# A two-layer hybrid trunk: the normalised input of the zm, gp and gm projections is formed once more from the reloaded residual

## The chip, the cores and the metric

The kernel runs on one core of a Trainium2 chip. The metric is device time in microseconds (us) for one execution. The kernel before took 788.91 us, the median of three runs (788.84 to 789.22).

Five engines work side by side, each through its own instructions in order: TensorE (PE, with its weight loads listed as PEld), VectorE (DVE), ScalarE (ACT), GpSimd (POOL) and SyncE (SP, which here only issues transfers). They meet through semaphores; TensorE writes to accumulator banks (PSUM), from which VectorE or ScalarE take the result away.

## The reference

Two layers, 512 tokens and 16 meta tokens in front of them (528 in all), model width 1024:

```python
for l in range(DEPTH):                       # DEPTH = 2
    h = rmsnorm(h_res, norm_gain[l])         # x * inv * gain, inv = rsqrt(mean(x*x) + eps)
    proj = h @ w_in[l]
    u_pool, z_pool, c_q, c_kv, k_rope, z_mla, g_pool, g_mla = split(proj)   # 512, 512, 768, 256, 32, 512, 1024, 1024
    y_pool = (pool_mix(u_pool, ...) * silu(z_pool)) @ pool_w_up[l]
    o_mla = mla(c_q, c_kv, k_rope, ...)      # 8 heads, q and k normalised, causal softmax
    y_mla = (o_mla * silu(z_mla)) @ mla_w_up[l]
    merged = sigmoid(g_pool) * y_pool + sigmoid(g_mla) * y_mla
    h_res = h_res + merged @ w_out[l]
return h_res[:, N_META:]
```

All of it is fp32.

## The kernel before

**Layout and arithmetic.** Features lie on the 128 partitions and tokens along the free dimension. Layer 0 computes 528 tokens in two segments of 264 (`FULL`), layer 1 only the 512 real tokens where it can (`XTOK`). Each fp32 operand of a projection is split into a high and a low half, and `mm3` (lines 184 to 187) makes each product of three matmuls: high by high (L185), low by high (L186), high by low weight (L187).

**The trunk.** `register` lists the projections of a layer in order, as `Gemm` entries: ckv, cq, u, k, v, zp (the pool branch's z), y, qr and qn (the query projection), pu0 to pu7 (the pool branch's up projection), zm0 to zm3 (the latent attention's z), gp and gm (the two gates, eight blocks each), mu (the attention's up projection) and o. The generator `stream` emits their matmuls. The weights come through `wload` (L170 to 182): a 256 KB transfer on SP's queue into one of three `raw` buffers, the high half by ScalarE (L180), the low half by VectorE (L181), three buffers of each.

**Order.** A planner clock `clk` counts the emitted matmuls at their nominal time. `fill_now(ns)` emits trunk matmuls until the clock has moved by ns, `upto(name)` until a projection is done, and `after(ns, fn)` puts work off to a due time. The source order that results is handed to a scheduler, which reorders each engine's instructions by a simulated timeline, within their dependencies.

**The norm.** `hbuf` (tiles hh and hl) holds the split of gain times x, without the factor `inv`, one value for each token. The factor is known only later (slot `rinv`, spread over the partitions), so it is applied when a result leaves PSUM. Three evacuations of the projections behind the query projection do so: `ev_silu` for zm (L505 multiplies by 0.5 and `inv`, ScalarE takes tanh, VectorE forms (tanh + 1) times that), `ev_gp` (L573: VectorE multiplies by `inv` into a temporary, ScalarE takes tanh of half of it, VectorE multiplies the pool branch's `am`), and `ev_gm` (L873 and ScalarE's tanh in place, into slot cq0 to cq7). The PSUM tiles that they read carry the tag mm (four banks); there are three of tag S and one o.

**Behind the query projection.** In `go`, after qn3, `qk_stats` (L665) sums the squares of queries and keys: matmuls into two S banks (`stat_go`, L453), `stat_rows` (ScalarE copy L463, VectorE add L464, once for each half of the tokens), 2.6 us of trunk, five small transposes on TensorE (L674, L675) and a Newton iteration on VectorE. Then 9.5 us of trunk, another 2.6, and `prep(0)`, which forms head 0's key (VectorE L701, GpSimd L702, the split L276 and L277 on ScalarE and VectorE) and moves parts of the query (L712). Then come the eight heads, with trunk matmuls filled in between: pu, zm, gp and part of gm. `part2` (L828) multiplies a head pair's output by zm, `meta_out` (L863) does so for the meta tokens, `ev_mu` (L877 ff.) joins the gates, `ev_o` forms the new residual and writes it to `scr` in memory and, in layer 0, to `xb`.

Slots cq0 to cq5 hold the query latent until the query projection has read it (cq6 and cq7 hold earlier squares), and later gm's gates.

Of the kernel before, what the change touches and what calls it, by code (L numbers as in the profile page):

```python
# [9 lines left out]
F32 = mybir.dt.float32  # L10
# [3 lines left out]
AF = mybir.ActivationFunctionType  # L14
ALU = mybir.AluOpType
# [3 lines left out]
P = 128  # L19
DEPTH = 2  # L20
D = 1024
SEQ = 512
NM = 16
T = SEQ + NM
# [13 lines left out]
MT_ZP = 6  # L38
MT_CQ = 10
MT_GP = 16  # L40
MT_ZM = 24
# [8 lines left out]
G_H, G_CKV, G_CQ, G_QN, G_QR, G_KN, G_KR, G_PS = 0, 8, 10, 16, 17, 18, 19, 20  # L50
# [21 lines left out]
def trunk(ctx, tc, xT, pos, win, wkr, wqb, wkb, wvb, wgr, wpu, wmu, wout, gains, const, yT):  # L72
    nc = tc.nc
    pe, act, dve, gp, sp = nc.tensor, nc.scalar, nc.vector, nc.gpsimd, nc.sync
# [7 lines left out]
    pp = ctx.enter_context(tc.tile_pool(name="pp", bufs=1, space=bass.MemoryType.PSUM))  # L82
# [3 lines left out]
    def nm(s):  # L86
        uid[0] += 1
        return f"{s}_{uid[0]}"

    def slot(tag, dt=F32, bufs=1, w=W):  # L90
        return sl.tile([P, w], dt, tag=tag, name=nm(tag), bufs=bufs)

    def tmp(w=W):
        return tp.tile([P, w], F32, tag="tmp", name=nm("tmp"), bufs=3)
# [1 line left out]
    def sqt():  # L96
        return tp.tile([P, HALF], F32, tag="sq", name=nm("sq"), bufs=14)

    def mmt():
        return pp.tile([P, 512], F32, tag="mm", name=nm("mm"), bufs=4)  # L100

    def sct():
        return pp.tile([P, 512], F32, tag="S", name=nm("S"), bufs=3)

    FULL = [(0, HALF), (HALF, T)]
    XTOK = [(NM, T)]
# [3 lines left out]
    xb = cp.tile([P, 8, W], F32, name="xb")  # L110
# [80 lines left out]
    done = set()  # L191

    def stream():
        flat = [(g_, c) for g_ in plan for c in range(0, g_.width, 512)]
        flat[1], flat[2] = flat[2], flat[1]

        def load(i):
            g_, c = flat[i]
            n = min(512, g_.width - c)
            return wload(g_.src[:, c:c + n], n, g_.gain, g_.spare)  # L200

        ahead = []
        for i in range(4):
            ahead.append(load(i))
            yield 0.0
        for i, (g_, c) in enumerate(flat):
            w = ahead.pop(0)
            if i >= 3 and i + 1 < len(flat):
                ahead.append(load(i + 1))
            final = c + 512 >= g_.width  # L210
            if g_.body is not None:
                yield from g_.body(c // 512, w)
            else:
                xs = g_.xs()
                K = len(xs)
                if c == 0:
                    g_.pss = [g_.alloc() for _ in g_.segs]
                k0 = c // P
                for ps, (a, b) in zip(g_.pss, g_.segs):
                    n = b - a  # L220
                    for k in range(k0, min(K, k0 + 4)):
                        o = (k - k0) * P
                        mm3(ps[:, :n], w[0][:, o:o + P], w[1][:, o:o + P],
                            xs[k][0][:, a:b], xs[k][1][:, a:b], k == 0, k == K - 1)
                        if k < K - 1 and (k - k0) % 2 == 1:
                            yield 6 * (n / 2.4)
                    if final:
                        g_.evac(ps[:, :n], a, b)
                        if b == g_.segs[-1][1]:
                            done.add(g_.name)  # L230
                        yield 6 * (n / 2.4)
            if final:
                done.add(g_.name)

    clk = [0.0]
    pend = []

    def step():
        c = next(main, None)
        if c is None:  # L240
            flush()
            return False
        clk[0] += c
        while pend and pend[0][0] <= clk[0]:
            pend.pop(0)[1]()
        return True
# [22 lines left out]

    def fill_now(ns):  # L270
        end = clk[0] + ns
        while clk[0] < end and step():
            pass

# [31 lines left out]
    scr = dp.tile([P, 8, SEQ], F32, name="scr")  # L306
# [6 lines left out]
    class Layer:  # L313
# [182 lines left out]
                dve.tensor_mul(self.us[m][:, NM + a:NM + b], ps, self.inv[:, a:b])  # L496
            return ev

        def ev_silu(self, dst, tag, m):
            def ev(ps, a, b):  # L500
                if a == self.x0:
                    dst[m] = slot(f"{tag}{m}") if tag == "u" else xb[:, m]
                d = dst[m][:, a:b]
                t = tmp()
                dve.scalar_tensor_tensor(out=d, in0=ps, scalar=0.5, in1=self.inv[:, a:b],  # L505
                                         op0=ALU.mult, op1=ALU.mult)
                act.activation(t[:, :b - a], d, AF.Tanh)
                dve.scalar_tensor_tensor(out=d, in0=t[:, :b - a], scalar=1.0, in1=d, op0=ALU.add, op1=ALU.mult)
            return ev

        def window(self, m):
# [58 lines left out]
        def ev_gp(self, m):  # L570
            def ev(ps, a, b):
                t = tmp()
                dve.tensor_mul(t[:, :b - a], ps, self.inv[:, a:b])  # L573
                act.activation(t[:, :b - a], t[:, :b - a], AF.Tanh, scale=0.5)
                dve.scalar_tensor_tensor(out=self.am[m][:, a:b], in0=t[:, :b - a], scalar=1.0,
                                         in1=self.am[m][:, a:b], op0=ALU.add, op1=ALU.mult)
            return ev
# [85 lines left out]
            return ev  # L663

        def qk_stats(self):  # L665
            fill_now(LAG + 100)
            self.stat_go(7)
            sts = self.stat_rows(self.x0)
            if self.last:
                dve.memset(sts[0:H, 0:NM], 1.0)  # L670
            fill_now(2600)
            stp = mmt()
            for j in range(4):
                pe.transpose(stp[:, H * j:H * j + H], sts[0:H, NM + P * j:NM + P * (j + 1)], ident[0:H, 0:H])  # L674
            pe.transpose(stp[0:NM, 4 * H:5 * H], sts[0:H, 0:NM], ident[0:H, 0:H])  # L675
            na, ny, nt = (sm.tile([P, 5, H], F32, tag=t, name=nm(t)) for t in ("na", "ny", "nt"))
            dve.memset(na[:, 4, :], 1.0)
            dve.tensor_scalar(self.eps, self.eps, EPS, None, op0=ALU.mult)
            eps = self.eps.unsqueeze(2).to_broadcast([P, 5, H])
            for r, j, k in ((P, 0, 4), (NM, 4, 5)):  # L680
                dve.scalar_tensor_tensor(out=na[0:r, j:k, :], in0=stp[0:r, H * j:H * k].rearrange("p (a b) -> p a b", b=H),
                                         scalar=1.0 / QK, in1=eps[0:r, j:k, :], op0=ALU.mult, op1=ALU.add)
            newton(ny, na, nt)
            self.nqs = sm.tile([P, 5, H], F32, tag="nqs", name=nm("nqs"))
            dve.tensor_scalar(self.nqs, ny, -1.0 / math.sqrt(QK), None, op0=ALU.mult)
            fill_now(9500)
            if not self.last:
                self.smeta = sm.tile([NM, 8, NM], F32, tag="smeta", name=nm("smeta"))

# [89 lines left out]
        def pv(self, prev, js):  # L779
# [3 lines left out]
            p, odd = h // 2, h % 2  # L783
# [8 lines left out]
            for j in js:  # L792
# [7 lines left out]
                out = ops[:, P * j:512]  # L800
# [17 lines left out]
            if odd == 1:  # L818
                op = self.op
                mt = self.mt  # L820

                def part2():
                    th, m = mt, mmt()
                    pe.matmul(m, self.vb[:, P * p:P * (p + 1)], th[0:96, 0:512], start=True, stop=True)
                    self.ogs[p] = (slot(f"q{p}", F32R), slot(f"kn{p}", F32R))
                    f = op[:, NM:T]
                    dve.tensor_add(f, m, f)
                    dve.tensor_mul(f, f, self.zms[p][:, NM:T])  # L828
                    split(*self.ogs[p], f, NM, T)

                after((3 if p == 3 else 2) * LAG, part2)
# [30 lines left out]

        def meta_out(self, p):  # L863
            f = tmp()
            dve.tensor_mul(f[:, 0:NM], self.mo[:, NM * p:NM * (p + 1)], self.zms[p][:, 0:NM])
            split(*self.ogs[p], f[:, 0:NM], 0, NM)

        def ev_gm(self, m):
            def ev(ps, a, b):
                if a == self.x0:  # L870
                    self.gms[m] = slot(f"cq{m}")
                d = self.gms[m][:, a:b]
                dve.tensor_mul(d, ps, self.inv[:, a:b])  # L873
                act.activation(d, d, AF.Tanh, scale=0.5)
            return ev

        def ev_mu(self, m):  # L877
# [31 lines left out]
        def register(self, nxt):  # L909
            l, XS = self.l, self.XS  # L910
            wi = lambda t: win[l, t]
            hs, ys, cs = (lambda: self.hs), (lambda: self.ys), (lambda: self.cs)

            def add(name, src, width, **kw):
                plan.append(Gemm((l, name), src, width, **kw))
# [16 lines left out]
                    add("kr", wkr[l], 256, body=self.kr_body, gain=gn[:, l * N_GAIN + G_H:l * N_GAIN + G_H + 8])  # L932
                kk(m)
            def zp(m):
                add(f"zp{m}", wi(MT_ZP + m), D, evac=self.ev_silu(self.zps, "xa", m), xs=hs, segs=XS)

            def y(m):
                add(f"y{m}", wgr[l, m], P, evac=self.ev_y(m), xs=lambda: [self.ys[m]], segs=XS)
# [15 lines left out]
            for m in range(8):  # L954
                add(f"pu{m}", wpu[l, m], 512, evac=self.ev_pu(m), xs=ys, segs=XS)
            for m in range(4):
                add(f"zm{m}", wi(MT_ZM + m), D, evac=self.ev_silu(self.zms, "u", m), xs=hs, segs=XS)
            for m in range(8):
                add(f"gp{m}", wi(MT_GP + m), D, evac=self.ev_gp(m), xs=hs, segs=XS)
            for m in range(8):  # L960
# [12 lines left out]
        def go(self, nxt):  # L973
# [29 lines left out]
                self.stat(self.acc[:, a0:b], a0, b, C_CQ, self.acc_last)  # L1003
            up("qn3")
            self.qk_stats()
            fill_now(2600)
            kq = self.prep(0)
            fill_now(2600)
            due[0] = None
# [100 lines left out]
```

## Time and profile before

| | |
|---|---|
| median of three runs | 788.91 us (788.84 to 789.22) |
| span of the profiled execution | 787.1 us |
| instructions | 14567 |
| matmuls on TensorE | 5301 |
| bytes moved by transfers | 81.83 MB |

The span goes from the first to the last instruction of one profiled execution; the median also has what lies around it. "Busy" is time in which an engine executes; the tenths of 40 slices show where in the span. A row of instructions reads: line of the kernel and engine, operation, result <- operands by the program's names, partitions x elements, how many, then busy time, mean duration in ns, and the idle time just before them with what ended most of it. A row of a timeline reads: start, duration, engine and line, operation, and in brackets a wait and what released it. A row by windows reads: the window, its length, and for each engine (TensorE, its weight loads, VectorE, ScalarE, GpSimd) the busy time and, in parentheses, the instructions; then the granted clock, the share of the transfers and their GB/s. A row of transfers ends with the KB of each and the median us from issue to landing.

Layer 0's last result leaves PSUM in a 0.42 us instruction that starts at 403.84 us (VectorE, L898); layer 1 takes the rest. The query projection's last evacuation (ScalarE, L661) starts at 149.85 us in layer 0 and at 542.8 us in layer 1.

### The profile page before, as it was taken

To read this page: it belongs to the slowest core of one execution; us is meant where nothing else is said; L and a number is where in the kernel's file an instruction comes from. 1 tells how busy PE (TensorE), PEld (TensorE's weight loads), DVE (VectorE), ACT (ScalarE), POOL (GpSimd) and SP (SyncE) were. 2 spreads that over 40 slices of the span, in tenths; PEclk is the share of its full clock that TensorE was granted. 3 is DMA by queue.
4 is the path that set the end of the run, shared out by engine and by line. 5 is a ranking of instruction groups with operands and counts; after the bars stand their busy time and mean duration, and the time that the engine had idled before them with its cause. 6 is when DMAs were issued, how large, how long until landed. Compare 5 with 4: busy or idle time off the path is not lost.

```text
span 787.1 us, 14567 instructions
## 1 busy us (share of the span) xinstructions
PE 780.9 (99%) x5301; PEld 708.6 (90%) x5301; DVE 535.1 (68%) x1165; ACT 410.8 (52%) x930; POOL 194.4 (25%) x259
## 2 busy tenths in 40 slices
PE   9999999999999999999999999999999999999998
PEld 8999899999999999999997898887788888887887
DVE  5848787446779987675464487775467888755932
ACT  7645655635656565633354356455445666554420
POOL 1034504002333242051000145131022333410500
PEclk9999999999999999999999999999999999999999
DMA  6242333423223212224642422334232222122372
GB/s 242 82 102 85 96 120 102 128 81 94 96 76 92 78 58 78 95 81 146 192 123 94 95 88 90 129 88 136 96 105 88 95 84 82 65 81 67 102 242 84
DMA packets 52263, 81.83 MB, mean 104 GB/s; under 512 B 8784, under 2 KB 17360, under 8 KB 52192
## 3 DMA queue, kind: packets, MB, share of 16 engines
q1 hardware_dynamic: 52048, 80.65, 32.9%
q8 instruction: 41, 0.67, 0.4%
q14 instruction: 30, 0.25, 0.1%
q10 hardware_dynamic: 144, 0.26, 0.1%
HBM read 74.49 MB, written 4.27 MB: 100 GB/s over the span
## 4 chain that ended last, share of the span: by engine, by line
PE 95%; DMA 2%; DVE 1%; issue 1%; ACT 0%; SPq 0%; ACTq 0%
PE mm L185 28%; PE mm L187 28%; PE mm L186 28%; PE mm L796 2%; PE S L186 2%; PE S L187 1%; PE S L185 1%; PE o L802 1%; PE o L801 1%; PE S L453 1%; DMA xb<-xT 1%; PE mm L355 1%; DVE wlo L181 1%; PE mm L412 0%; DMA rinv<-win 0%
## 5 line engine op out<-in xcount | busy, mean ns | idle before, releaser
L185 PE MATMUL mm<-hh,whi 128*128 128x264 f32 (+2 forms) x1096 | 346.7, 318 | 0.2 <-ACT racc L810 0.2
L186 PE MATMUL mm<-hl,whi 128*128 128x264 f32 (+2 forms) x1096 | 343.9, 315 | 0.0
L187 PE MATMUL mm<-hh,wlo 128*128 128x264 f32 (+2 forms) x1096 | 343.0, 315 | 0.0
L181 DVE TENSOR_TENSOR wlo<-raw,whi 128x512 fp32r<-128x512 f32 (+2 forms) x251 | 188.6, 755 | 119.6 <-ACT whi L180 115.9
L180 ACT ACTIVATE whi<-raw 128x512 fp32r<-128x512 f32 (+2 forms) x251 | 150.4, 601 | 187.5 <-PE mm L186 126.5
L185 PEld LDWEIGHTS mm<-hh,whi 128*128 128x128 f32 x1096 | 205.9, 188 | 13.6 <-ACT racc L810 0.5
L186 PEld LDWEIGHTS mm<-hl,whi 128*128 128x128 f32 x1096 | 206.6, 189 | 11.8
L187 PEld LDWEIGHTS mm<-hh,wlo 128*128 128x128 f32 x1096 | 205.5, 188 | 12.0
L774 POOL TENSOR_TENSOR pm<-pa,rs 128x16 f32<-128x16 f32 x32 | 11.6, 361 | 181.3 <-DVE rs L769 181.3
L560 POOL TENSOR_TENSOR racc<-racc,tmp 128x264 f32<-128x264 f32 (+1 forms) x15 | 14.2, 948 | 153.8 <-ACT tmp L559 129.8
L702 POOL TENSOR_TENSOR tmp<-kp,bc 64x528 f32<-64x528 f32 x16 | 22.5, 1408 | 76.9 <-PE mm L675 44.5
L884 POOL TENSOR_TENSOR tmp<-tmp,xb 128x264 f32<-128x264 f32 (+1 forms) x24 | 27.1, 1149 | 58.2 <-DVE tmp L882 33.1
L730 DVE CUSTOM_DVE_ANT_0 S<-S,maskw,nqs 128x272 f32<-128x272 f32 (+4 forms) x80 | 38.5, 498 | 4.2 <-PE S L187 3.9
L737 ACT ACTIVATE cq<-S,bia 128x400 f32<-128x400 f32 (+2 forms) x48 | 24.6, 516 | 22.6 <-DVE bia L764 12.0
L185 PE MATMUL mm<-u,whi 128*128 128x264 f32 (+1 forms) x108 | 35.2, 326 | 0.0
L187 PE MATMUL mm<-cq,wlo 128*128 128x264 f32 (+1 forms) x108 | 34.5, 323 | 0.7 <-DVE wlo L181 0.7
L187 PE MATMUL mm<-u,wlo 128*128 128x264 f32 (+1 forms) x108 | 34.8, 323 | 0.0
L185 PE MATMUL mm<-cq,whi 128*128 128x264 f32 (+1 forms) x108 | 34.6, 320 | 0.0
L186 PE MATMUL mm<-cq,whi 128*128 128x264 f32 (+1 forms) x108 | 34.5, 321 | 0.0
L277 DVE TENSOR_TENSOR tl<-mm,th 128x512 fp32r<-128x512 f32 (+1 forms) x64 | 29.3, 481 | 6.1 <-ACT th L276 5.1
L776 POOL TENSOR_TENSOR cq<-cq,rs 128x384 f32<-128x384 f32 (+1 forms) x32 | 32.8, 1025 | 0.0
L186 PE MATMUL mm<-kn,whi 128*128 128x264 f32 (+1 forms) x96 | 30.7, 321 | 0.0
(252 smaller groups left out, 1362.4 us busy)
## 6 DMA issues: line engine op xcount, KB each, us to landing
raw<-win SPq DMA_DIRECT2D x143, 256.0 KB, 2.6
raw<-wout SPq DMA_DIRECT2D x32, 256.0 KB, 2.7
bc<-kdr SPq DMA_DIRECT2D x16, 264.0 KB, 3.6
raw<-wpu SPq DMA_DIRECT2D x16, 256.0 KB, 2.7
raw<-wmu SPq DMA_DIRECT2D x16, 256.0 KB, 2.5
raw<-wqb SPq DMA_DIRECT2D x12, 256.0 KB, 2.6
tmp<-xT SPq DMA_DIRECT2D x16, 132.0 KB, 3.0
tmp<-scr SPq DMA_DIRECT2D x7, 256.0 KB, 3.4
```

The source lines that it names most:

```text
L180: act.activation(hi[:, :n], raw[:, :n], AF.Copy)
L181: dve.tensor_sub(lo[:, :n], raw[:, :n], hi[:, :n].bitcast(F32))
L185: pe.matmul(out, wh, xh, start=start, stop=False)
L186: pe.matmul(out, wh, xl, start=False, stop=False)
L187: newest[0] = pe.matmul(out, wl, xh, start=False, stop=stop)
L277: dve.tensor_sub(lo[:, a:b], src, hi[:, a:b].bitcast(F32))
L702: gp.tensor_mul(kf[r0:r0 + 64, :], self.kp[r0:r0 + 64, :], bc[r0:r0 + 64, :])
L730: dve.tensor_tensor_reduce(out=sv, in0=sv, in1=mask, scale=nqs[:, i, h:h + 1], scalar=3e38, op0=ALU.add, op1=ALU.min, accum_out=bia[:, c:c ...
L737: act.activation(pv, sv, AF.Exp, scale=-1.0, bias=bia[:, i:i + 1], accum_out=rs[:, c:c + 1])
L776: gp.tensor_mul(pt[i][:, NM:], pt[i][:, NM:], rs[:, i:i + 1].to_broadcast([P, n - NM]))
L796: pe.transpose(tr[:, P * (i - j):P * (i - j + 1)], pt[i][:, NM + P * j:NM + P * (j + 1)], ident)
L884: gp.tensor_add(t[:, :b - a], t[:, :b - a], self.am[m][:, a:b])
```

## The change

After the query projection the kernel reads its input again: x in layer 0 (`xT`), the stored residual in layer 1 (`scr`), one block of 128 features at a time into slots cq0 to cq7. It multiplies each block by `inv` and splits gain times that into the same hh and hl tiles. This is the new method `renorm`: per block one transfer on SP, a multiply on VectorE, a copy with gain on ScalarE and a subtract on VectorE. In the source six blocks come at the end of `qk_stats`, in place of its 9.5 us of trunk, and two behind it, in place of 2.6 us; they are set to planner times from the start of `qk_stats` (6.0 us and 1.5 us more for each block), through the new `fill_to`.

From zm on, the projections therefore come out normalised. The evacuations of gp and gm drop their multiply by `inv`, and ScalarE takes tanh from PSUM. That of zm takes tanh from PSUM and then forms (tanh + 1) times the PSUM value on VectorE; the factor 0.5, which used to lie in it, moves to the two places that read zm. PSUM tiles of the trunk are named by their projection.

```diff
+    def fill_to(end):
+        while clk[0] < end and step():
+            pass
...
+        def renorm(self, ks):
+            x0 = self.x0
+            assert (self.l, "pu7") not in done
+            for k in ks:
+                x = slot(f"cq{k}")
+                src = xT[:, k, x0:T] if self.l == 0 else scr[:, k, :]
+                sp.dma_start(x[:, x0:T], src)
+                x, (hh, hl), gk = x[:, x0:T], self.hs[k], self.g(G_H + k)
+                dve.tensor_mul(x, x, self.inv[:, x0:T])
+                act.activation(hh[:, x0:T], x, AF.Copy, scale=gk)
+                dve.scalar_tensor_tensor(out=hl[:, x0:T], in0=x, scalar=gk, in1=hh[:, x0:T].bitcast(F32),
+                                         op0=ALU.mult, op1=ALU.subtract)
+
+        def ev_zm(self, m):
+            def ev(ps, a, b):
+                if a == self.x0:
+                    self.zms[m] = slot(f"u{m}")
+                t = tmp()
+                act.activation(t[:, :b - a], ps, AF.Tanh, scale=0.5)
+                dve.scalar_tensor_tensor(out=self.zms[m][:, a:b], in0=t[:, :b - a], scalar=1.0, in1=ps,
+                                         op0=ALU.add, op1=ALU.mult)
             return ev
...
         def ev_gp(self, m):
             def ev(ps, a, b):
                 t = tmp()
-                dve.tensor_mul(t[:, :b - a], ps, self.inv[:, a:b])
-                act.activation(t[:, :b - a], t[:, :b - a], AF.Tanh, scale=0.5)
+                act.activation(t[:, :b - a], ps, AF.Tanh, scale=0.5)
...
         def qk_stats(self):
+            self.t0 = clk[0]
             fill_now(LAG + 100)
...
-            fill_now(9500)
+            for k in range(6):
+                fill_to(self.t0 + 6000 + 1500 * k)
+                self.renorm((k,))
...
                     dve.tensor_add(f, m, f)
-                    dve.tensor_mul(f, f, self.zms[p][:, NM:T])
+                    dve.scalar_tensor_tensor(out=f, in0=f, scalar=0.5, in1=self.zms[p][:, NM:T],
+                                             op0=ALU.mult, op1=ALU.mult)
...
         def meta_out(self, p):
             f = tmp()
-            dve.tensor_mul(f[:, 0:NM], self.mo[:, NM * p:NM * (p + 1)], self.zms[p][:, 0:NM])
+            dve.scalar_tensor_tensor(out=f[:, 0:NM], in0=self.mo[:, NM * p:NM * (p + 1)], scalar=0.5,
+                                     in1=self.zms[p][:, 0:NM], op0=ALU.mult, op1=ALU.mult)
...
         def ev_gm(self, m):
             def ev(ps, a, b):
                 if a == self.x0:
                     self.gms[m] = slot(f"cq{m}")
-                d = self.gms[m][:, a:b]
-                dve.tensor_mul(d, ps, self.inv[:, a:b])
-                act.activation(d, d, AF.Tanh, scale=0.5)
+                act.activation(self.gms[m][:, a:b], ps, AF.Tanh, scale=0.5)
             return ev
...
-                add(f"zm{m}", wi(MT_ZM + m), D, evac=self.ev_silu(self.zms, "u", m), xs=hs, segs=XS)
+                add(f"zm{m}", wi(MT_ZM + m), D, evac=self.ev_zm(m), xs=hs, segs=XS)
...
             self.qk_stats()
-            fill_now(2600)
+            for k in (6, 7):
+                fill_to(self.t0 + 6000 + 1500 * k)
+                self.renorm((k,))
             kq = self.prep(0)
```

More of the change, by code (lines that the diff above doesn't have):

```diff
@@ L97, in sqt, with mmt, sct @@
         return tp.tile([P, HALF], F32, tag="sq", name=nm("sq"), bufs=14)
[L99 to L103, printed above, removed]
+    def mmt(name="mm"):
+        return pp.tile([P, 512], F32, tag="mm", name=nm(name), bufs=4)
+    def sct(name="S"):
+        return pp.tile([P, 512], F32, tag="S", name=nm(name), bufs=3)
     FULL = [(0, HALF), (HALF, T)]
@@ L216, in stream @@
                 if c == 0:
-                    g_.pss = [g_.alloc() for _ in g_.segs]
+                    g_.pss = [g_.alloc(g_.name[1]) for _ in g_.segs]
                 k0 = c // P
@@ L497, in ev_u, with ev_silu @@
             return ev
-        def ev_silu(self, dst, tag, m):
+        def ev_silu(self, dst, m):
             def ev(ps, a, b):
                 if a == self.x0:
-                    dst[m] = slot(f"{tag}{m}") if tag == "u" else xb[:, m]
+                    dst[m] = xb[:, m]
                 d = dst[m][:, a:b]
@@ L508, in ev @@
                 dve.scalar_tensor_tensor(out=d, in0=t[:, :b - a], scalar=1.0, in1=d, op0=ALU.add, op1=ALU.mult)
+            return ev
+        def renorm(self, ks):
[18 more added lines that the diff above has]
+                                         op0=ALU.add, op1=ALU.mult)
             return ev
@@ L934, in zp @@
             def zp(m):
-                add(f"zp{m}", wi(MT_ZP + m), D, evac=self.ev_silu(self.zps, "xa", m), xs=hs, segs=XS)
+                add(f"zp{m}", wi(MT_ZP + m), D, evac=self.ev_silu(self.zps, m), xs=hs, segs=XS)
             def y(m):
```

## The prediction

> **What bounds the kernel now.** I read the page first: the span, the first row of busy times, the clock row and the shares of the chain that ended last.
>
> ```profile
> span 787.1 us, 14567 instructions
> PE 780.9 (99%) x5301; PEld 708.6 (90%) x5301; DVE 535.1 (68%) x1165; ACT 410.8 (52%) x930; POOL 194.4 (25%) x259
> PEclk9999999999999999999999999999999999999999
> PE 95%; DMA 2%; DVE 1%; issue 1%; ACT 0%; SPq 0%; ACTq 0%
> ```
>
> TensorE sets the time from end to end, at an undisturbed clock. Whether any slack hides in its 99% is told by how many matmuls pass per stretch; here is one stretch among the heads and one of the last projection, of the view by windows.
>
> ```profile
> 220.00:240.00 20.00, 20.00 (x165) 19.77 (x163) 17.24 (x41) 10.61 (x26) 7.80 (x10) 1.00 0.26 87
> 380.00:400.00 20.00, 20.00 (x166) 20.00 (x166) 7.88 (x14) 7.19 (x12) 0.00 (x0) 1.00 0.61 186
> ```
>
> Both pass one matmul in 0.12 us (20/165, 20/166), the first with VectorE 86% busy, the second with it 39% busy. So a lighter VectorE buys nothing among the heads. What TensorE waits for at all, in the whole run:
>
> ```profile
> PE mm L187 <- DVE wlo L181: 0.7, 1, 0.7
> PE mm L185 <- DVE tmp L882: 0.3, 1, 0.3
> PE mm L185 <- ACT racc L810: 0.2, 1, 0.2
> ```
>
> (The rest of that view lies in the first 13 us.) The first is the second layer's query projection, ahead of the change's place. So the gain to be had is about a microsecond, and the question is what the reload adds to TensorE's path.
>
> **What is removed.** The evacuation of gp and gm loses its VectorE multiply by the norm factors; that of zm keeps one VectorE instruction of two.
>
> ```profile
> L873 DVE TENSOR_TENSOR cq<-mm,rinv 128x264 f32<-128x264 f32 x16 | 6.9, 429 | 2.4 <-PE mm L187 2.3
> L573 DVE TENSOR_TENSOR tmp<-mm,rinv 128x264 f32<-128x264 f32 x16 | 6.7, 424 | 0.3
> ```
>
> Each group has eight more of 512 columns in the second layer (0.69 us, as wlo of 512 below), so 12.3 us each, and zm's twelve some 6 us: about 31 us of VectorE work, all under matmuls at their floor: worth 0 by itself. What it can free is an accumulator bank that TensorE waits for. The two places are:
>
> ```profile
> 338.18 0.28 PE L187 MATMUL mm<-q,wlo 128*128 128x264 f32 x1
> 338.75 0.39 PE L185 MATMUL mm<-q,whi 128*128 128x264 f32 x1 [0.28 <-DVE tmp L882]
> ...
> 708.38 0.39 PE L187 MATMUL mm<-hh,wlo 128*128 128x512 f32 x1
> 708.87 0.47 PE L801 MATMUL o<-th,vt 128*128 128x512 f32 x1
> 709.54 0.50 PE L185 MATMUL mm<-hh,whi 128*128 128x512 f32 x1 [0.21 <-ACT racc L810]
> ```
>
> Start to start, less the pace (0.12 us for 264 columns, 0.23 for 512): 0.45 at 338.75, 0.26 and 0.44 at 708.87 and 709.54; together 1.1 us. In the order of the built program the waiting matmul of mu2 stands three matmuls behind the one whose result it waits to be taken away, in the changed one seven; the other place no longer stands so close. I take all of it as saved: −1.1, with bounds of 0 and of −1.9 (the wlo wait too).
>
> **What is added: work ahead of a transpose that TensorE must pass.** Per layer: 8 DMAs on SP's queue, 8 multiplies (L523 of the new file) and 8 subtracts (L525) on VectorE, 8 copies (L524) on ScalarE. The scheduler has not put them behind qk_stats, where the source has them, but ahead of its second half. VectorE's order in layer 0 of the changed program:
>
> ```
> L523 cq0; L181 wlo (pu2); L523 cq1; L523 cq2; L525 hl0; L523 cq3; L525 hl1; L523 cq4;
> L181 wlo (pu3); L525 hl2; L523 cq5; L525 hl3; L523 cq6; L730 (key of head 0); L525 hl4;
> L468 tmp<-S, first half; L468 second half; L523 cq7; ...
> ```
>
> L468 is the old L464: it feeds the five transposes of qk_stats, and the first of these still stands right behind pu1 (layer 0) or pu2 (layer 1) on TensorE, ahead of pu2 or pu3 and of all later matmuls. In layer 0 head 0's first score matmul, which needs the key copy (ScalarE, behind six of the new copies), has been moved up to that place too. TensorE waits there until the chain above is through. Where the place is now, and what leads to it:
>
> ```profile
> 146.54 0.29 PE L187 MATMUL mm<-cq,wlo 128*128 128x264 f32 x1
> ...
> 157.26 0.22 PE L674 MATMUL mm<-cst,tmp 8*128 8x8 f32 x1
> ...
> 538.57 0.40 PE L187 MATMUL mm<-cq,wlo 128*128 128x512 f32 x1
> ...
> 552.84 0.22 PE L674 MATMUL mm<-cst,tmp 8*128 8x8 f32 x1
> ```
>
> The reload of cq0 waits for the last matmul that reads the latent in that buffer. Counted back in the built order from pu0's first matmul these are the rows at 146.54 and 538.57, done at 146.83 and 538.97. The transfer:
>
> ```profile
> raw<-wpu SPq DMA_DIRECT2D x16, 256.0 KB, 2.7
> tmp<-scr SPq DMA_DIRECT2D x7, 256.0 KB, 3.4
> xb<-xT SPq DMA_DIRECT2D x2, 264.0 KB, 3.4
> ```
>
> 2.7 us beside the same weight loads, 3.4 in a burst (the last row is of the first 20 us); I take 2.9, nearer to the first since cq0 leads its own burst: VectorE begins at 149.73 and 541.87. Its steps:
>
> ```profile
> 152.88 0.69 DVE L181 TENSOR_TENSOR wlo<-raw,whi 128x512 fp32r<-128x512 f32 x1 [2.19 <-ACT whi L180]
> 153.49 0.69 DVE L701 TENSOR_TENSOR tmp<-kn,bc 64x528 f32<-64x528 f32 x1
> 155.48 0.89 DVE L464 TENSOR_TENSOR tmp<-S,tmp 8x264 f32<-8x264 f32 x2 [1.30 <-ACT tmp L463]
> ...
> 186.62 0.69 DVE L277 TENSOR_TENSOR kl<-tmp,kh 128x528 fp32r<-128x528 f32 x1
> 187.29 0.69 DVE L181 TENSOR_TENSOR wlo<-raw,whi 128x512 fp32r<-128x512 f32 x1
> ...
> 400.18 2.13 DVE L338 SCALAR_TENSOR_TENSOR hl<-xb,gn,hh 128x528 fp32r<-128x528 f32 x3 [1.32 <-ACT hh L336]
> ```
>
> Back to back, starts are nearer than durations: 0.61 us for 512 columns (153.49 − 152.88), 0.67 for 528 (187.29 − 186.62); a subtract like L525 takes (2.13 − 0.76)/2 = 0.68, with 0.76 the one of L338 alone. For L523, which the trace lacks, I take 0.64, between 0.61 and 0.67. Layer 0: 7 × 0.64 + 5 × 0.68 + 2 × 0.61 + 0.61 + 0.45 (half of L464's pair) = 10.2, so the transpose can start at 149.73 + 10.2 = 159.9 and not at 157.26: **+2.6**. The key copy is ready a little earlier (multiply for the key done 1.1 us before, ScalarE 0.64 a copy). Layer 1, with the order cq1, cq0, wlo, cq3, ..., has from cq0 to the transpose 7 multiplies at 0.61 (512 columns), 7 subtracts at 0.67, 4 weight splits, the key's multiply and one L468: 4.3 + 4.7 + 2.4 + 0.6 + 0.4 = 12.4, so 554.3 and not 552.84: **+1.5**. Behind the waiting instruction stands every later matmul, so both go straight into the time: the weight splits of pu2 and pu3 come before the end of the wait, and the zm projection, which needs the new halves, starts over 15 us later.
>
> The Trainium skill (VectorE: DVE Perf Modes, The DRAIN you can't avoid) says that the next instruction doesn't start before the pipeline of the last has emptied. By it each step would cost its whole duration (0.71, 0.76, 0.69), layer 0 would lose 3.5 and layer 1 2.6, and the time would be 793.8; the rows at 152.88 and 153.49, 0.61 apart at 0.69 long, speak for the smaller figure.
>
> Bounds of the two waits: all steps at 0.61 and landing in 2.7 us gives 1.8 + 0.9 = 2.7; full durations and landing in 3.5 gives about 4.5 + 3.3 = 7.8.
>
> **What lies beside other work.** SP's queue now holds the reloads ahead of the weights of pu4 to pu7; three raw buffers cover that, and the two stretches have room:
>
> ```profile
> 149.20:157.30 8.10, 8.10 (x79) 6.69 (x77) 3.31 (x6) 4.41 (x12) 0.00 (x0) 1.00 0.50 132
> 542.70:552.80 10.10, 10.10 (x63) 7.18 (x62) 4.24 (x7) 4.86 (x12) 0.00 (x0) 1.00 0.46 131
> ```
>
> DMA is half busy there and VectorE 41%. Without that cover a weight would be late by one reload, about 1 us. The two factors of 0.5 that move to L857 and L895 swap a multiply for one of the same operands: 0.
>
> **Sum.** −1.1 + 2.6 + 1.5 = +3.0 on the span of 787.1, so 790.1; what lies around the span is 788.91 − 787.1 = 1.8, so 791.9.
>
> **Rivals.** *One wait alone (790.4).* Layer 1's lead is longer (cq1 can start 0.9 us before cq0) and its wait the smaller; if it vanishes, −1.1 + 2.6 = +1.5. *Both hidden (787.8), not slower.* This needs the chain from cq0's landing to the transpose to take less than 157.26 − 149.73 = 7.5 us in layer 0, or TensorE to run pu2, whose operands are ready, past the waiting transpose. Sixteen instructions in 7.5 us is 0.47 each, below any row above. The Trainium skill (TensorE: Matmul & The Clock Gate, Part 3, The mechanism) says that matmuls start and end strictly in program order; the wait at 709.54 with ready hh matmuls behind it agrees. *Reloads land late (797.9).* The burst at the start of the kernel shows it:
>
> ```profile
> DMA packets 2305, 4.77 MB, mean 239 GB/s; under 512 B 384, under 2 KB 512, under 8 KB 2304
> raw<-win SPq DMA_DIRECT2D x7, 256.0 KB, 5.0
> xb<-xT SPq DMA_DIRECT2D x3, 528.0 KB, 5.9
> ```
>
> If the reloads land in 5.9 us instead of 2.9, each layer waits 3 us more: 791.9 + 6. It decides once a landing passes the 1.3 us per block at which VectorE asks for blocks; 264 KB at 239 GB/s is 1.1 us, so it is close. *The change doesn't do what it says* would be rows of L505, L573 and L873 still there; the built program has none.
>
> **Chances.** Forecast 0.62, one wait 0.14, both hidden 0.07, late reloads 0.17. The range goes from the lower bound with the larger saving (788.9 + 2.7 − 1.9, 789.7, taken down to 789.4 for the second rival with the larger saving) to 797.0 (7.8 of waits and nothing saved). A difference of 0.2% (1.6 us) is about what a measurement can tell here. Slower by more than that, over 790.5: nearly all of the forecast's and the late reloads' chance, a little of the second, 0.77; within it 0.18; faster 0.05.
>
> **What would show it.** TensorE's waits gain one entry per layer on the transposes L701 (or the first score matmul), near 157 and 553, of 2 to 3 and 1 to 2 us; elsewhere it passes 165 matmuls in 20 us as now; the waits on L882 and racc are gone; L523 and L525 fill VectorE from about 149.7 and 541.9. I am wrong if these waits are absent, if they sit on a wlo (late weights), or if TensorE is held among the heads.

## The result, and the profile after

The changed kernel takes 798.11 us (median of four, 796.97 to 799.22) beside 789.07 us before (four, 788.84 to 789.97). The ratio is 1.011, with an interval of 1.0097 to 1.0122. It is slower by 9.0 us; the forecast was 3.0 us, and the time lies above the range.

The page of the changed kernel: span, busy times, granted clock, chain by engine.

```profile
span 796.6 us, 14557 instructions
PE 785.2 (99%) x5301; PEld 712.4 (89%) x5301; DVE 529.2 (66%) x1137; ACT 418.2 (52%) x946; POOL 194.5 (24%) x259
PEclk9999999989999999999999999999999999999999
PE 93%; DVE 3%; DMA 2%; issue 1%; ACT 0%; SPq 0%; ACTq 0%; DVEq 0%
```

The span is 9.5 us longer with as many matmuls as before. VectorE is less busy and yet has 3% of the chain now. And the row of clocks has an 8 in its ninth slice, where before there were only nines.

TensorE's waits, whole view but for the start-up:

```profile
PE mm L701 <- DVE tmp L468: 3.7, 1, 3.7
PE S L185 <- ACT kh L280: 2.5, 1, 2.5
...
PE qn L187 <- DVE wlo L181: 0.7, 1, 0.7
```

There is one new wait in each layer, at the place that the prediction names: in layer 0 at head 0's first score matmul, in layer 1 at the first transpose. The waits on L882 and on racc (L810) are gone. The two new ones come to 6.2 us, less than the 9.5. The rest is in the view by windows: first layer 0's wait, what follows it in two pieces of 6.82 us, then layer 1's wait and the stretch behind it. After the window and its length come TensorE, its weight loads, VectorE, ScalarE, GpSimd, then the granted clock.

```profile
157.56:160.11 2.55, 0.00 (x1) 0.01 (x1) 2.52 (x5) 2.49 (x5) 0.00 (x0) 0.94 0.20 73
159.80:166.62 6.82, 6.51 (x29) 5.98 (x30) 5.11 (x11) 1.38 (x3) 1.80 (x1) 0.50 0.27 78
166.62:173.44 6.82, 6.82 (x58) 6.82 (x58) 3.60 (x16) 2.91 (x7) 0.00 (x0) 1.00 0.26 77
557.94:561.60 3.66, 0.00 (x0) 0.00 (x1) 3.60 (x7) 2.23 (x4) 0.00 (x0) 1.00 0.43 117
562.57:565.98 3.41, 3.41 (x10) 2.64 (x9) 1.32 (x3) 0.00 (x0) 1.32 (x1) 0.50 0.51 135
```

TensorE is idle for 2.55 us, and from 159.80, 0.31 us before it goes on, the clock stands at 0.50 for 6.83 us: 29 matmuls pass where the next 6.82 us pass 58. In layer 1 3.67 us of idle time, to 561.60, are followed by 3.41 us at 0.50, from 562.57 on. TensorE counts as busy there (6.51 of 6.82), so neither the 99% nor the view of waits shows it, and in the row of slices the second stretch is lost: half the clock for 3.41 us of a 19.9 us slice leaves 0.91, which prints as 9.

A stretch at half clock costs at most half its length: 3.41 and 1.71 us. With the waits that is at most 2.55 + 3.67 + 3.41 + 1.71 = 11.3 us, where the span grew by 9.5. What the two stretches do cost is measured with busy3 below: 2.74 and 1.60 us.

The key copy on ScalarE, which ended layer 0's wait, and the two chains on VectorE (timeline: start, duration, line, operation), layer 0's up to 159.95, layer 1's from 547.62 on:

```profile
159.42 0.63 ACT L280 ACTIVATE kh<-tmp 128x528 fp32r<-128x528 f32 x1
...
150.04 0.71 DVE L523 TENSOR_TENSOR cq<-cq,rinv 128x528 f32<-128x528 f32 x1 [0.61 <-DMA cq<-xT]
150.67 0.68 DVE L181 TENSOR_TENSOR wlo<-raw,whi 128x512 fp32r<-128x512 f32 x1
151.46 1.38 DVE L523 TENSOR_TENSOR cq<-cq,rinv 128x528 f32<-128x528 f32 x2
...
158.54 0.69 DVE L730 TENSOR_TENSOR tmp<-kn,bc 64x528 f32<-64x528 f32 x1
159.16 0.75 DVE L525 SCALAR_TENSOR_TENSOR hl<-cq,gn,hh 128x528 fp32r<-128x528 f32 x1
159.95 0.89 DVE L468 TENSOR_TENSOR tmp<-S,tmp 8x264 f32<-8x264 f32 x2
...
547.62 0.69 DVE L523 TENSOR_TENSOR cq<-cq,rinv 128x512 f32<-128x512 f32 x1 [2.06 <-DMA cq<-scr]
549.14 0.69 DVE L523 TENSOR_TENSOR cq<-cq,rinv 128x512 f32<-128x512 f32 x1 [0.82 <-DMA cq<-scr]
...
561.14 0.88 DVE L468 TENSOR_TENSOR tmp<-S,tmp 8x248 f32<-8x248 f32 x2
```

Layer 0's chain begins at 150.04 (forecast 149.73) and its transpose could start at about 160.4 (forecast 159.9). In layer 1 cq0's multiply starts at 549.14, and from there it is 12.46 us to the transpose at 561.60 (forecast 12.4). So the lengths of both chains were right; layer 1's began late, at a place where the transfers fill 93.5% of the DMA engines' time:

```profile
DMA packets 1359, 2.49 MB, mean 311 GB/s; under 512 B 148, under 2 KB 148, under 8 KB 1358
q1 hardware_dynamic: 1358, 2.48, 93.5%
...
DMA to landing us min/median/max: 2.9/5.1/6.4
```

The first two rows are of 543 to 551 us, the last of all sixteen reloads. Three weight loads for pu were issued between 541.59 and 543.00, cq1 at 543.10 and cq0 at 543.92; cq0 landed at 549.04, 5.1 us after its issue, where the prediction took 2.9; in layer 0 cq0 did land in 2.9. (All of layer 1 stands 4.9 us later than in the prediction's working, 543.92 for 538.97, because layer 0 has lost that much; this is no part of the landing.)

One execution of all those below, the first of busy2 (1076.11 us), ran at a granted clock of 0.65 to 0.75 nearly from end to end and is left out of the times; in its trace stretches at 0.50, of 3.41 and 6.83 us, stand right behind the filling matmuls though TensorE does not wait there, and nothing here explains them.

### The profile page after: what moved, and what is told of

It reads as the page before. It is cut to its first block, busy times and chain, and to the rows that moved or that the text cites. A ratio compares the mean times of both kernels' runs of the same rounds, so it can differ in the third digit from the quotient of the medians.

```text
span 796.6 us, 14557 instructions
## 1 busy us (share of the span) xinstructions
PE 785.2 (99%) x5301; PEld 712.4 (89%) x5301; DVE 529.2 (66%) x1137; ACT 418.2 (52%) x946; POOL 194.5 (24%) x259
## 4 chain that ended last, share of the span: by engine, by line
PE 93%; DVE 3%; DMA 2%; issue 1%; ACT 0%; SPq 0%; ACTq 0%; DVEq 0%
PE gm L185 4%; PE gp L185 4%; PE gp L187 4%; PE gm L186 4%; PE gp L186 4%; PE gm L187 4%; PE o L187 4%; PE o L185 4%; PE o L186 4%; PE cq L185 3%; PE cq L187 3%; PE cq L186 3%; PE mm L825 2%; PE u L185 2%; PE u L187 2%; PE u L186 2%
## 5 line engine op out<-in xcount | busy, mean ns | idle before, releaser
L185 PE MATMUL gp<-hh,whi 128*128 128x264 f32 (+1 forms) x192 | 63.0, 329 | 0.0
L187 PE MATMUL o<-hh,wlo 128*128 128x264 f32 (+2 forms) x200 | 63.0, 315 | 0.0
L185 PE MATMUL o<-hh,whi 128*128 128x264 f32 (+2 forms) x200 | 62.8, 314 | 0.0
L185 PE MATMUL gm<-hh,whi 128*128 128x264 f32 (+1 forms) x192 | 62.8, 329 | 0.0
L186 PE MATMUL o<-hl,whi 128*128 128x264 f32 (+2 forms) x200 | 62.8, 314 | 0.0
L187 PE MATMUL gp<-hh,wlo 128*128 128x264 f32 (+1 forms) x192 | 61.8, 323 | 0.0
L186 PE MATMUL gp<-hl,whi 128*128 128x264 f32 (+1 forms) x192 | 61.8, 322 | 0.0
L187 PE MATMUL gm<-hh,wlo 128*128 128x264 f32 (+1 forms) x192 | 61.8, 322 | 0.0
L186 PE MATMUL gm<-hl,whi 128*128 128x264 f32 (+1 forms) x192 | 61.7, 322 | 0.0
L185 PE MATMUL cq<-hh,whi 128*128 128x264 f32 (+1 forms) x144 | 46.4, 324 | 0.0
```

The source lines that it names most:

```text
L185: pe.matmul(out, wh, xh, start=start, stop=False)
L186: pe.matmul(out, wh, xl, start=False, stop=False)
L187: newest[0] = pe.matmul(out, wl, xh, start=False, stop=stop)
```

## Experiments

Two explanations stand for the half clock. A: an idle TensorE is itself followed by a stretch at half clock. B: the reload's own work beside the matmuls slows them.

**Hold the multiplies behind the Newton iteration (later).**

```diff
-            dve.tensor_scalar(self.nqs, ny, -1.0 / math.sqrt(QK), None, op0=ALU.mult)
+            self.turned = dve.tensor_scalar(self.nqs, ny, -1.0 / math.sqrt(QK), None, op0=ALU.mult)
...
-                dve.tensor_mul(x, x, self.inv[:, x0:T])
+                behind(dve.tensor_mul(x, x, self.inv[:, x0:T]), self.turned)
```

> The changed kernel, with the multiplies of the reload held until the Newton iteration's result (nqs) is there, behind the transposes. Theory A (the changed kernel loses 2.55 and 3.67 us to two waits ahead of the transposes and some 4.8 us to the half clock that follows each wait): both waits and both stretches of half clock vanish, the saved bank waits of some 1.5 us stay, about 787.5 us. Rival B (the half clock comes from the reload's own work beside the matmuls, not from the wait): the waits vanish and the slow stretches stay, about 792.3 us. Against both: the late halves hold up the zm projection, which would show as TensorE waits on hh or hl of zm.

Measured: 787.61 us (786.49 to 788.22), 789.60 before on the same chip; ratio 0.9974 (0.9962 to 0.9987). Span 785.0, clock 1.0. It has the whole reload and beats both kernels. Its VectorE and TensorE timelines around layer 0's transposes:

```profile
155.32 0.89 DVE L468 TENSOR_TENSOR tmp<-S,tmp 8x264 f32<-8x264 f32 x2 [1.30 <-ACT tmp L467]
163.34 0.18 DVE L712 TENSOR_SCALAR nqs<-ny 128x40 f32<-128x40 f32 x1
163.56 5.04 DVE L523 TENSOR_TENSOR cq<-cq,rinv 128x528 f32<-128x528 f32 x8
```
```profile
157.10 0.22 PE L701 MATMUL mm<-cst,tmp 8*128 8x8 f32 x1
```

L468 is back in its old place, the transpose runs at 157.10 without a wait, and the eight multiplies pass in one go behind 163.34, 14 us ahead of the first zm matmul at 177.6. B's 792.3 is excluded.

**The reload in layer 0 held, in layer 1 not (later0).**

```diff
-                behind(dve.tensor_mul(x, x, self.inv[:, x0:T]), self.turned)
+                made = dve.tensor_mul(x, x, self.inv[:, x0:T])
+                if self.l == 0:
+                    behind(made, self.turned)
```

> The changed kernel, with the reload's multiplies held behind the Newton iteration in layer 0 only. The two losses are separate: layer 0 loses nothing, layer 1 keeps its wait of 3.7 us and 3.4 or 6.8 us of half clock (1.7 or 3.4 us of loss): 787.6 + 3.7 + 1.7 to 3.4, so 793.0 to 794.7 us. If layer 1's wait came from layer 0's delay it would vanish too: 787.6 us.

Measured: 793.40 us (792.14 to 795.56); ratio 1.0051 (1.0033 to 1.0069). Layer 1 alone waits, 3.67 us, and this time the stretch at half clock is 6.83 us long; it begins at 554.67, inside the wait (552.29 to 555.96). The two layers' losses are separate.

**The evacuations alone (noreload).** The loop of `renorm` runs over nothing.

> The changed kernel without the reload (transfers, multiplies, copies and subtracts of renorm left out, so zm, gp and gm come out without the factor inv): the cheaper evacuations alone. By the waits that are gone in the changed kernel (mu2 of layer 0, pv of layer 1) 787.5 us, no wait at the transposes, clock 1.00. If the evacuations themselves cost something, it is over 788.9 us.

Measured: 787.36 us (786.97 to 788.59); ratio 0.9974 (0.9964 to 0.9984), span 785.5, which is 1.6 us under before. That is all there is to gain from the lighter evacuations, and later, which reloads everything, has it too (787.61): held in the right place, the reload costs nothing that can be measured.

**The reload alone (reloadonly).** The multiplies by `inv` put back into the evacuations of zm, gp and gm.

> The changed kernel with the old evacuations of zm, gp and gm put back (multiply by inv as before, so these results carry the factor twice): the reload alone. Theory A: the two waits and two clock drops as in the changed kernel, without the 1.5 us saved, 799.5 us. Rival: the lighter evacuations shape the waits too, and the time is within 1 us of the kernel before.

Measured: 798.46 us (797.31 to 799.39); ratio 1.0109 (1.0094 to 1.0124), span 797.6. Waits of 2.81 and 3.67 us, half clock of 6.83 and 3.41 us, as in the changed kernel.

**TensorE kept busy through the wait (busy, busy2, busy3).**

```diff
+            idle = pp.tile([P, 512], F32, tag="o", name=nm("idle"), bufs=1)
+            for j in range((20, 30)[self.l]):
+                behind(pe.matmul(idle[:, 0:P], identr, identr, start=True, stop=True), self.summed)
             stp = mmt()
```

`self.summed` is the last matmul of the query sums. The first try had 44 and 62.

> The changed kernel, with 44 (layer 0) and 62 (layer 1) matmuls of 128 columns, which nothing reads, ahead of the first transpose, about 2.5 and 3.5 us of TensorE work in place of the idle time. Theory A: the transposes come at the same time as in the changed kernel but the clock stays at 1.00, so about 4.8 us less, 793.3 us. Rival B: no change beside the changed kernel, 798.1 us, with half clock at the same places.

Measured: 799.52 us (798.66 to 800.28), ratio 1.0123 (1.0108 to 1.0138), but at clock 1.00. The 44 matmuls took 5.02 us and the 62 7.04, 0.114 us each and twice what I had counted on, so 12.1 us of work stood in place of 6.2 us of idle time. That is 5.9 us more, and 4.3 less for the clock (by busy3, below), so 1.6 us of the 1.9 by which its span, 798.5, is the longer; the rest isn't placed. This kernel tells the theories apart by its clock, not by its time. So with 20 and 30:

> As busy, but 20 and 30 matmuls that nothing reads, now sized by their measured 0.114 us: 2.3 and 3.4 us, so that they end before the transposes' operand is there. Theory A: transposes at the time of the changed kernel, what is left of the idle time under 1 us each, no stretch at half clock, so the changed kernel's 798.1 less the 5.1 us that its two stretches (6.83 and 3.41 us at half clock) cost: 793.0 us. Rival B (the slow stretches come from the reload's own work): 798.1 us with half clock.

> The same kernel as busy2, for an undisturbed trace. Theory A: no stretch at half clock, 106.. the waits' place filled by 20 and 30 matmuls of 0.114 us with under 1 us of idle time behind each, time between 793.0 us (the changed kernel less 5.1) and the 796.0 us of busy2's undisturbed executions; what lies above 793.0 shows as idle time or extra matmul time at the two places, or in the start-up. Rival B: half clock at the two places.

Measured: busy2 794.40 to 796.18 us in three executions, ratio 1.0075 (1.0058 to 1.0092); busy3 796.37 us (795.07 to 796.60) beside 790.20 before, ratio 1.0076 (1.006 to 1.0091). The trace of busy3, by windows: the matmuls in layer 0's wait and the stretch behind them, then the same in layer 1.

```profile
158.13:160.47 2.34, 2.34 (x22) 2.20 (x20) 2.34 (x5) 2.27 (x6) 0.00 (x0) 1.00 0.42 115
161.11:167.94 6.83, 6.83 (x54) 6.49 (x55) 6.75 (x15) 2.43 (x5) 1.81 (x1) 1.00 0.31 78
555.03:558.49 3.46, 3.46 (x32) 3.46 (x31) 3.46 (x6) 1.65 (x4) 0.00 (x0) 1.00 0.24 76
559.87:566.70 6.83, 6.83 (x33) 5.38 (x33) 4.75 (x17) 2.87 (x6) 1.72 (x1) 1.00 0.45 130
```

The second row is the point: VectorE is busier with the reload (6.75 of 6.83 us) than in the changed kernel, and 54 matmuls pass in 6.83 us, where that had 29. The reload's work doesn't slow TensorE; B falls.

The trace also gives the price of the two stretches, since the same matmuls stand between two places in both kernels. First the changed kernel, then busy3: 161 matmuls from head 0's first scores to the first of zm in layer 0, 74 from the first transpose to the first of zm in layer 1.

```profile
160.11 0.59 PE L185 MATMUL S<-kh,qhl 128*128 128x272 f32 x1 [2.55 <-ACT kh L280]
182.78 0.28 PE L185 MATMUL zm<-hh,whi 128*128 128x264 f32 x1
561.60 0.22 PE L701 MATMUL mm<-cst,tmp 8*128 8x8 f32 x1 [3.67 <-DVE tmp L468]
579.14 0.39 PE L185 MATMUL zm<-hh,whi 128*128 128x512 f32 x1
...
161.11 0.39 PE L185 MATMUL S<-kh,qhl 128*128 128x272 f32 x1 [0.64 <-ACT kh L280]
181.04 0.28 PE L185 MATMUL zm<-hh,whi 128*128 128x264 f32 x1
559.87 0.22 PE L705 MATMUL mm<-cst,tmp 8*128 8x8 f32 x1
575.81 0.39 PE L185 MATMUL zm<-hh,whi 128*128 128x512 f32 x1
```

Layer 0 takes 22.67 us for 19.93, layer 1 17.54 for 15.94: the stretches cost 2.74 and 1.60 us, 4.34 together and not the 5.1 expected. The span, 793.3, is 3.3 under the changed kernel's: busy3 comes to the first scores 1.0 us later (161.11 for 160.11) and gains 4.34 behind them.

**A wait without any reload (wait_a to wait_e).** The kernel before, with a chain of multiplications by 1.0 ahead of the transposes, of a length for each layer, and the next 60 products of the trunk held behind the transposes (`hold`) so that the scheduler doesn't fill the gap:

```diff
+            for _ in range((5, 12)[self.l]):
+                dve.tensor_scalar(sts[0:H, 0:T], sts[0:H, 0:T], 1.0, None, op0=ALU.mult)
             stp = mmt()
...
-            pe.transpose(stp[0:NM, 4 * H:5 * H], sts[0:H, 0:NM], ident[0:H, 0:H])
+            hold[:] = [pe.transpose(stp[0:NM, 4 * H:5 * H], sts[0:H, 0:NM], ident[0:H, 0:H]), 60]
```

> The kernel before, with 5 (layer 0) and 12 (layer 1) multiplications by 1.0 of the query sums in a chain on VectorE ahead of the transposes, and the trunk matmuls held behind these: a wait of TensorE without any reload. At some 0.4 us each, less the 1.0 us of slack, waits of about 1.0 and 3.8 us. Theory A (an idle TensorE is itself followed by a stretch at half clock): the 3.8 us wait is followed by 3 to 6 us at 0.50 as in the changed kernel, costing 1.6 to 3.2 us beyond the wait; the 1.0 us wait, shorter than any that was followed by one, by none. Rival B (the reload's work slows the matmuls): clock 1.00 throughout, loss = waits alone.

> As wait_a with 7 and 9: waits of about 1.8 and 2.6 us. Theory A: half clock behind the second (2.55 us was enough in the changed kernel's layer 0); the first tells whether less is enough. Rival B: clock 1.00.

> As wait_a with 9 and 7: waits of about 2.6 and 1.8 us, the same lengths in the other layer. Theory A: half clock behind the first, at least; if what decides is only the length, the 1.8 us wait does as in wait_b. If it hangs on when the wait begins, the two kernels differ. Rival B: clock 1.00.

> As wait_a with 12 and 5: waits of about 3.8 and 1.0 us. Theory A: half clock behind the first and none behind the second, total loss 1.6 to 3.2 us above the waits. Rival B: clock 1.00.

> As wait_a with 3 and 2 multiplications: by the 0.46 us that each took there, waits of some 1.6 and 1.8 us. Theory A with the bound seen so far (2.47 us of idle time was once followed by no half clock, 2.55 us and more always by 3.41 or 6.83 us of it): clock 1.00 in all executions, loss = waits, 789.1 + 3.4 = 792.5 us. If the stretches come whatever the length, the clock is 0.996 or less and the time 794 us or more.

Times: 799.63, 801.33, 801.82, 802.11 us (one each, 789.33 before), and wait_e 792.14 us (nine, 790.37 to 793.61), ratio 1.003 (1.0019 to 1.004). In wait_a to wait_d there was less slack than I had taken, so the waits came out longer than expected. In wait_e they came out shorter, 1.07 and 1.27 us for 1.6 and 1.8. Its trace stays at clock 1.00, and its time is as expected; but in three of the nine executions the mean clock is 0.997 or 0.998, where the twelve of the kernel before have 0.999 or 1.0. One stretch of 3.41 us would make 0.998, so that a wait of this length is never followed by one isn't shown. By windows, the wait and what follows it; wait_a:

```profile
157.50:159.97 2.47, 0.00 (x0) 0.03 (x1) 2.29 (x5) 0.87 (x2) 0.00 (x0) 1.00 0.03 12
159.97:166.80 6.83, 6.83 (x58) 6.79 (x59) 4.23 (x17) 2.10 (x5) 1.34 (x1) 1.00 0.25 70
553.98:560.33 6.35, 0.00 (x1) 0.00 (x1) 5.92 (x14) 0.34 (x1) 0.00 (x0) 0.87 0.10 27
558.65:565.48 6.83, 5.15 (x16) 4.16 (x17) 5.59 (x20) 1.23 (x2) 1.30 (x1) 0.50 0.01 2
```

wait_c:

```profile
157.43:161.73 4.30, 0.00 (x0) 0.03 (x1) 3.98 (x9) 0.87 (x2) 0.00 (x0) 1.00 0.19 62
161.88:165.29 3.41, 3.41 (x19) 3.37 (x19) 2.80 (x11) 0.10 (x1) 1.33 (x1) 0.50 0.00 0
```

No reload, and the half clock is there: A is shown from this side too. The new waits of 1 us and more, by trace:

| kernel, layer | wait, us | at half clock, us |
|---|---|---|
| wait_e, 0 and 1 | 1.07, 1.27 | none |
| fromxb, 1 (below) | 2.07 | 3.41 |
| wait_a, 0 | 2.47 | none |
| fromxb, 0 (below) | 2.50, then 0.69 | 3.41 |
| changed kernel, 0 | 2.55 | 6.83 |
| reloadonly, 0 | 2.81 | 6.83 |
| wait_d, 1 | 3.15 | 3.41 |
| wait_b, 0 | 3.39 | 6.83 |
| changed kernel, 1; reloadonly, 1 | 3.67 | 3.41 |
| later0, 1 | 3.67 | 6.83 |
| wait_c, 1 | 4.07 | 6.83 |
| wait_c, 0 | 4.30 | 3.41 |
| wait_b, 1 | 4.98 | 6.83 |
| wait_d, 0 | 5.68 | 6.83 |
| wait_a, 1 | 6.35 | 6.83 |

**Half of the transfers (fromxb).** Blocks 4 to 7 still stand in `xb`; they are taken from there, first, without a transfer.

```diff
-                sp.dma_start(x[:, x0:T], src)
+                if k < 4:
+                    sp.dma_start(x[:, x0:T], src)
...
-                dve.tensor_mul(x, x, self.inv[:, x0:T])
+                dve.tensor_mul(x, x if k < 4 else xb[:, k, x0:T], self.inv[:, x0:T])
...
-                self.renorm((k,))
+                self.renorm(((k + 4) % 8,))
```

> The changed kernel, but blocks 4 to 7 are taken from xb, which still holds them, and come first: half of the reload's transfers are gone, and VectorE's chain begins without a landing. If the late landing (5.1 us in layer 1) makes the wait of 3.67 us as long as it is, layer 1's chain starts 3 to 4 us earlier and its wait falls under 1 us, layer 0's likewise; without half clock 787.5 to 789.5 us. If VectorE's queue alone makes the waits, they stay near 2.5 and 3.7 us and the time near 798 us.

Measured: 797.08 us (795.19 to 797.55), ratio 1.0091 (1.0076 to 1.0106): a miss. Its VectorE chains did start earlier:

```profile
147.91 2.56 DVE L524 TENSOR_TENSOR cq<-xb,rinv 128x528 f32<-128x528 f32 x4 [1.15 <-PE qn L186]
...
160.84 0.89 DVE L468 TENSOR_TENSOR tmp<-S,tmp 8x264 f32<-8x264 f32 x2
...
545.44 1.28 DVE L524 TENSOR_TENSOR cq<-xb,rinv 128x512 f32<-128x512 f32 x2
```

But in layer 0 the scheduler used the two microseconds to put all sixteen steps of the reload ahead of L468 (sixteen and not twelve), and L468 came at 160.84, later than the changed kernel's 159.95; waits of 2.50 and 0.69 us. Only in layer 1 did the wait shrink, from 3.67 to 2.07 us, and not to under 1 us. VectorE's order makes both waits; how much of layer 1's is the landing this run doesn't show by itself, since it changes that order too.

A kernel with both edits, later's and fromxb's (later_xb, expected within 0.5 of 787.6 us or up to 0.5 faster than later), took 788.97 us (787.88 to 791.20) beside 790.20 before, ratio 0.9984 (0.9973 to 0.9994), without a wait at the transposes. But its results are not the layers': it reads blocks of `xb` at 166.6 us (L524) that the evacuation of pu has been writing to since 151.3 us (L595). So it settles nothing about the transfers.

## Why the prediction was wrong, point by point

- **That TensorE's path gains a wait at the transposes, and why.** Right: place, sign and cause. The work that the scheduler put ahead of L468 is the cause, since moving it behind (later) removes both waits, and lighter evacuations with no reload (noreload) have none.
- **Layer 0, +2.6.** Right: 2.55. The wait ended with the key copy (ScalarE, done at 160.05), for head 0's first scores, which stand ahead of the transposes on TensorE, and not with the sums that the forecast went by: their first half was done at about 160.4, 0.5 us later than forecast. So the mechanism held, and a little luck brought the number so close.
- **Layer 1, +1.5.** Too small: 3.67. One term was mis-sized, cq0's landing: 5.1 us instead of 2.9, at a place where DMA is 93.5% busy. I took the landing "nearer to the first since cq0 leads its own burst", which held in layer 0; in layer 1 three weight loads and cq1 led it. 5.1 − 2.9 = 2.2, and 1.5 + 2.2 = 3.7. The rival of late reloads named this, for both layers, at 3 us each; it came true in one. Its 5.9 us were those of 528 KB transfers; the row of the right size in the same fence, raw<-win of 256 KB at 5.0, was close to the measured 5.1.
- **"both go straight into the time".** This step failed. It prices a wait at its own length, and so did the bounds: full durations and late landing gave 7.8 and the top of the range. Here each of these waits was also followed by a stretch at half clock, 2.74 + 1.60 = 4.3 us, about half of the 9.0 lost. With this step put right, the forecast's own waits would have been priced at 2.6 to 5.3 us and at 1.5 to 3.1 (the table has nothing between 1.27 us, without a stretch, and 2.07 us, with one): an estimate of 791.9 to 796.2 us. To come to 798.1 it takes the landing too.
- **The saving of 1.1.** Right, a little small: 1.6 by noreload's span. The wait on wlo at the query projection (0.7) stayed.
- **Covered work.** Right: no weight split became late, TensorE is at its pace among the heads, the two factors of 0.5 cost nothing that shows.
- **Two figures of the working** don't come out, and nothing hangs on them: whole durations make 11.3 us of steps in layer 0 and a loss of 3.8, not 3.5; and the single wait with the larger saving gives 789.6 as the lower end, not 789.4.

| term | forecast, us | shown, us |
|---|---|---|
| wait in layer 0 | +2.6 | +2.55 |
| wait in layer 1 | +1.5 | +3.67 |
| half clock behind them | none | +4.34 |
| bank waits saved | −1.1 | −1.6 |
| sum | +3.0 | +9.0 (span: +9.5) |

Of the 0.5 us left, 0.3 lie in how a wait is counted: from start to start, less the pace, the two are 2.72 (157.27 to 160.11) and 3.83 (557.54 to 561.60). The other 0.2 I can't place.

The Trainium skill (TensorE: Matmul & The Clock Gate, Part 1) says that the clock falls to half behind an idle window of about 3.4 us, by a window that runs free; the warning stood on the very page that the prediction draws on for another point. The traces agree with the half and with the free window. They don't agree with 3.4 us as the idle time that is needed: 2.07 and 2.55 us were enough.

## What to carry to other kernels

Where TensorE sets the time, price a wait of some 2 us or more at its length plus about 1.6 to 2.7 us, and look at the clock in windows of a few us behind each wait: busy shares, slices and waits don't show it. When work is added that has much time before it is needed, see where the scheduler puts it on an in-order engine; here one dependency that held it behind the short chain to the transposes turned 1.1% slower into 0.3% faster.

## What the runs showed of the hardware

The 14 stretches at half clock of the table are 3.41 or 6.83 us long, and they begin on a fixed grid within an execution: 562.57 − 159.80 = 118.0 × 3.413 in the changed kernel, 559.64 − 160.28 = 117.0 × 3.413 in wait_b. In 13 of the 14 TensorE had been idle for 2.04 us or more of the 3.413 us just before; in wait_a's layer 0 the grid cut the wait of 2.47 us so that 1.79 us fell into one window, and no stretch followed. In one (wait_d, layer 1) 1.53 us were enough, so there is more to the rule than that sum.

The first 3.41 us of a stretch tell its length. In all eight stretches of 6.83 us TensorE was still idle for some of them (0.24 us in wait_b's layer 0 at the least, 0.31 in the changed kernel's); in all six of 3.41 us it was busy for all of them but 0.08 us at most. So a wait that ran on into the 3.41 us in which the clock had fallen was followed by as much again at half clock.

The grid lies differently from one execution to the next (a stretch begins at 159.80 in the changed kernel's trace, at 160.28 in wait_b's). That fits how the time moves from one execution to the next: the changed kernel's 796.97 and 797.81 us had a mean clock of 0.996, 798.40 had 0.994 and 799.22 had 0.993.

At half clock matmuls of 264 columns start 0.22 us apart (161.44 to 165.18 in the changed kernel) instead of 0.122, those of 512 columns 0.43 instead of 0.23: 1.8 times as slow, not twice, and so a stretch costs less than half its length.

A matmul of 128 columns by a 128 x 128 weight of its own took 0.114 us back to back, twice the quarter of a 512-column one (0.23 us) at which I had sized it: 5.02 us for 44.
